# Two projections of a mixer as one product in seven parts, with the order of its neighbours changed: an encoder kernel on one Trainium2 core

## The chip, the core and the metric

One NeuronCore of a Trainium2 chip runs the whole program. The metric is the device time of one execution in microseconds. Abbreviations as in the profile: PE is TensorE (matmuls; PEld its weight loads), DVE VectorE, ACT ScalarE, POOL GpSimd, SP SyncE; POOL and SP issue the DMAs here. "L178" is line 178 of the kernel.

## What is computed

Two layers, each a half-step feed-forward part (FFN), a mixer, and a second FFN, on x of 512 tokens by 1024 channels, float32 (hidden width 2816). The mixer, cut to what matters:

```python
h = rms_norm(x)
z = h @ w_in                      # q, k, v, uf: 512 columns each; ga, gf: 1024 each
y_na = neighbourhood_attention(q, k, v, rpb) @ w_na_out     # 8 heads of 64
y_f  = real(fft2(uf per group of 128 channels, over positions and channels)) @ w_f_out
x = x + (sigmoid(ga + b0) * y_na + sigmoid(gf + b1) * y_f) @ w_o
```

## The kernel before

**Precision and products.** Every float32 operand of a matmul is split in a high and a low part of a rounded type, and a product is three matmuls: high by high, high by low, low by high (`mm3` L285 to L288; the low part is made by `split`: ACT copies the high part, L292 or L295, DVE subtracts, L293 or L296). A matmul of 128x512 has 128 rows of output channels or tokens and 512 columns. The FFNs and the mixer's gates multiply 2x2 blocks with seven products in place of eight (Strassen's scheme, `product`, L447, L448, L450): each product is 24 matmuls of 128x512 into two PSUM banks, and sums and differences of x's blocks and of the weights' blocks are its operands.

**The weight stream.** All weights lie in DRAM as granules of 128x1024 float32 (512 KB), in a list in the order of use (`stage_items`). `Stream.fetch` issues their loads on SP's queue eight ahead (L144); sums of two granules are made by a second DMA that adds, on POOL's queue (L146, L180), or by DVE (L160). `prep` then makes the high part on ACT (`whi`, L175, negated L170) and the low part on DVE (`wlo`, L178, L171), three buffers of each, two granules ahead of PE.

**The mixer before the change.** `Norm.quad` transposes x on PE and splits each chunk from PSUM (L295, L296). `proj_U` computes u (the 512 Fourier columns) as it stands for the first half of the tokens and in reversed order for the second half, with reversed copies of x's parts on ACT and DVE (L986, L987) as operands: 96 matmuls of 128x512. `proj_V`: 96 more. Between them 1/rms comes by integer start and three Newton steps on DVE (`rsqrt`, L304 to L309), and `spread` sends it to all partitions by DRAM as R; `constants` loads the Fourier matrices by POOL's queue. Then, in program order: the bias and shifted-v loads (SP), `four_pos` for four groups (12 matmuls each; DVE multiplies by the rotations L1048, L1049, adds and subtracts L1050, L1051, then the split into b), q and k of head pair 0 (`proj_T`, 24 matmuls each, times R on DVE L970, split), `four_ch` for four groups (6 matmuls each, two PSUM banks each; ACT evicts `fq` L1063, DVE combines to `fy` L1065 to L1067, split into y L1071, L1072), q of pair 1, then the attention of four head pairs.

`att_next(hp)` transposes the probabilities of the pair before (`att_trans`, L1140, split into p), does the scores of pair hp (`att_scores`, 24 small matmuls, L1104), adds the bias and finds the maximum on DVE (L1118), takes Exp on ACT (L1124), the reciprocal of the sum on DVE (L1127) and scales on ACT (L1131). `att_outs(hp)` multiplies the transposed probabilities by v. `f_some(n)` does n of the eight row blocks of y_f (12 matmuls of 128x512 each, L1202 evicts; the first four rows read one pair of weight granules, the others a second). The order of these calls is:

```python
four_pos x4; q0; k0; four_ch x4; q1
att_next(0); k1; q2;  att_next(1); k2; att_outs(0); q3
att_next(2); k3; att_outs(1); f_some(2)
att_next(3); f_some(2); att_outs(2); f_some(1); att_next(4); f_some(2); ...
```

**What sets the order.** PE runs in program order, in effect. The queues of DVE and ACT are ordered by a scheduler in the framework, which places the instructions by their program order and its own reckoning of when operands are ready; inside `manual_schedule` blocks they stand as written. Each queue is strict: an instruction that waits holds up all behind it. PSUM has eight banks, given out in turn.

Of the kernel before, what the change touches and what calls it, by code (L numbers as in the profile page):

```python
# [17 lines left out]
P = 128  # L18
# [22 lines left out]
def _granules():  # L41
# [7 lines left out]
    for l in range(L):  # L49
        for w in (1, 2):  # L50
# [36 lines left out]
def encoder_kernel(  # L87
# [95 lines left out]
    def stage_items():  # L183
# [5 lines left out]
        def strassen(s, name, idx, sizes, order, dma=False):  # L189
# [7 lines left out]
            for m in order:  # L197
                for g in range(len(sizes)):
# [13 lines left out]
                    else:  # L212
                        add(c)

# [15 lines left out]
        for l in range(L):  # L230
# [4 lines left out]
            for name, n in (("u", 4), ("v", 4), ("qk", 8), ("f", 4)):  # L235
                for g in range(n):
                    add(Raw((s, name, g)))
# [11 lines left out]
    class Stream:  # L249
        def __init__(self):  # L250
            self.items = stage_items()
            self.pos = self.loaded = self.prepped = 0
            self.stage = 0

# [6 lines left out]
        def prep(self, to):  # L261
            n = len(self.items)
            while self.prepped < min(to, n) and self.items[self.prepped].stage <= self.stage:
                self.fetch(self.prepped + FETCH)
# [4 lines left out]
        def enter(self, stage):  # L269
            self.stage = stage  # L270
            self.fetch(self.prepped + FETCH)
# [40 lines left out]
    class Norm:  # L312
# [105 lines left out]
        def rstd(self):  # L418
# [101 lines left out]
    def less(ps, t):  # L520
        for b in range(2):
            V.tensor_tensor(t[:, b, :], ps[b], t[:, b, :], ALU.subtract)  # L522

    def stage_ffn(norm, nxt, late):
# [27 lines left out]
        norm.tiles(1)  # L552
# [16 lines left out]
        acts = {1: (hx[0], lx[0], 0), 2: (hx[1], lx[1], 0), 3: (hx[1], lx[1], 256), 4: (*t4, 0)}  # L569

        def combine(m):

            if m == 5:
                V.tensor_tensor(raw[0, 0], raw[0, 0], raw[0, 1], ALU.subtract)
                acts[5] = parts(raw[0, 0], "t1")
            elif m == 7:
# [1073 lines left out]
```

## Time and profile before

| what | us |
|---|---|
| median of three runs (lowest, highest) | 1905.98 (1905.19, 1907.02) |
| the profiled execution | 1906.04 |
| span in its profile | 1904.2 |
| PE busy | 1891.7 |
| first matmul of u, layer 0 | 337.15 |
| end of scores of head pair 0, layer 0 | 408.45 |
| its first transpose | 419.56 |

The profile is one execution. Its page gives the busy time of each engine, the span in 40 slices, the DMA queues, the chain that ended last, and the costliest groups of instructions; the trace behind it answers more: the waits of an engine with what released it, the busy time in given stretches, the instructions of a stretch in order of time. A line such as "383.30 0.69 DVE L1048 ..." has the start, the duration, the engine, the line, the operation, and its output and inputs. Matmuls, and most instructions of DVE and ACT, begin before the one ahead has ended, so the price of one in a full queue is the step from one start to the next.

### The profile page before, as it was taken

The numbers are of one execution on the slowest core, as the hardware profiler recorded it, in microseconds if no ns is written. First come the engines' busy times: TensorE is split into PE (matmuls) and PEld (weight loads), VectorE is DVE, ScalarE is ACT, GpSimd is POOL, SyncE is SP. The second block draws the span as 40 slices with busy tenths as digits, with TensorE's granted clock in tenths as the row PEclk, the third lists the DMA queues.
The fourth block names the chain that finished last, engine by engine and source line by source line (L and its number), as shares of the span: only waits on it lengthen the run. The fifth ranks groups of instructions, "written<-read, shape, count | busy, mean of one in ns | idle before, by whom it ended". The sixth has DMA issues, their size and how long they took to land.

```text
span 1904.2 us, 25091 instructions
## 1 busy us (share of the span) xinstructions
PE 1891.7 (99%) x9189; PEld 1586.8 (83%) x9189; DVE 1602.4 (84%) x2000; ACT 1161.6 (61%) x1676; POOL 160.7 (8%) x198
## 2 busy tenths in 40 slices
PE   9999999999999999999999999999999999999998
PEld 7888888888888888888888888888888888888886
DVE  7877899586889987889997778995769899787899
ACT  6655665468566755566665556663675576555655
POOL 0101010000111010001010100100001101000010
PEclk9999999999999999999999999999999999999999
DMA  8776499323886776649877664992247867766594
GB/s 301 202 207 187 150 249 320 105 84 104 217 218 166 180 195 204 177 152 262 251 185 210 187 180 152 268 339 74 68 130 215 215 170 175 207 177 177 170 275 147
DMA packets 104636, 364.36 MB, mean 191 GB/s; under 512 B 12032, under 2 KB 12160, under 8 KB 104512
## 3 DMA queue, kind: packets, MB, share of 16 engines
q1 hardware_dynamic: 77568, 270.70, 40.1%
q0 software_dynamic: 26800, 92.04, 26.8%
q8 instruction: 72, 1.18, 0.2%
q14 instruction: 52, 0.43, 0.1%
q10 hardware_dynamic: 144, 0.02, 0.0%
HBM read 357.46 MB, written 2.11 MB: 189 GB/s over the span
## 4 chain that ended last, share of the span: by engine, by line
PE 95%; issue 2%; DMA 2%; DVE 1%; ACT 0%; POOL 0%; DVEq 0%; ACTq 0%; POOLq 0%; SPq 0%
PE A L447 9%; PE A L448 9%; PE A L450 9%; PE o L448 7%; PE o L447 7%; PE o L450 7%; PE ps L286 5%; PE ps L288 5%; PE ps L287 5%; PE B L448 4%; PE B L447 4%; PE B L450 4%; PE C L448 2%; PE C L447 2%; PE C L450 2%; PE tr L540 2%
## 5 line engine op out<-in xcount | busy, mean ns | idle before, releaser
L175 ACT ACTIVATE whi<-raw 128x1024 fp32r<-128x1024 f32 (+1 forms) x528 | 546.1, 1037 | 423.4 <-PE A L448 123.2
L178 DVE TENSOR_TENSOR wlo<-raw,whi 128x1024 fp32r<-128x1024 f32 (+1 forms) x528 | 627.3, 1193 | 191.2 <-ACT whi L175 186.5
L146 POOL DMA_DIRECT2D raw<-in_wst_dram x158 | 136.2, 873 | 1440.2 <-DMA raw<-in_wst_dram 674.7
L160 DVE TENSOR_TENSOR raw<-raw,raw 128x1024 f32<-128x1024 f32 (+1 forms) x146 | 172.6, 1191 | 1.2
L448 PE MATMUL A<-whi,xl 128*128 128x512 f32 x384 | 149.5, 389 | 0.0
L447 PE MATMUL A<-whi,xh 128*128 128x512 f32 x384 | 149.4, 389 | 0.0
L450 PE MATMUL A<-wlo,xh 128*128 128x512 f32 x384 | 110.5, 389 | 0.0
L170 ACT ACTIVATE whi<-raw 128x1024 fp32r<-128x1024 f32 (+1 forms) x79 | 81.6, 1036 | 40.2 <-PE A L448 12.4
L171 DVE SCALAR_TENSOR_TENSOR wlo<-raw,whi 128x1024 fp32r<-128x1024 f32 (+1 forms) x79 | 93.1, 1193 | 12.2 <-ACT whi L170 12.2
L633 ACT ACTIVATE th<-sn,rh 128x512 f32<-128x512 f32 x80 | 56.8, 714 | 69.4 <-DVE sn L522 69.4
L517 ACT ACTIVATE sn<-A 128x512 f32<-128x512 f32 x96 | 56.4, 589 | 51.3 <-PE A L450 51.2
L450 PEld LDWEIGHTS A<-wlo,xh 128*128 128x128 f32 x384 | 72.1, 188 | 15.0
L448 PEld LDWEIGHTS A<-whi,xl 128*128 128x128 f32 x384 | 72.1, 188 | 14.8
L447 PEld LDWEIGHTS A<-whi,xh 128*128 128x128 f32 x384 | 72.1, 188 | 14.8
L447 PE MATMUL B<-whi,t1h 128*128 128x512 f32 x192 | 76.2, 397 | 0.0
L447 PE MATMUL A<-whi,t3h 128*128 128x512 f32 x192 | 75.3, 392 | 0.4 <-ACT sn L517 0.4
L447 PE MATMUL C<-whi,xh 128*128 128x512 f32 x192 | 74.9, 390 | 0.0
L447 PE MATMUL A<-whi,t2h 128*128 128x512 f32 x192 | 74.9, 390 | 0.0
L448 PE MATMUL B<-whi,t1l 128*128 128x512 f32 x192 | 74.8, 390 | 0.0
L448 PE MATMUL A<-whi,t3l 128*128 128x512 f32 x192 | 74.8, 390 | 0.0
L448 PE MATMUL C<-whi,xl 128*128 128x512 f32 x192 | 74.7, 389 | 0.0
L448 PE MATMUL A<-whi,t2l 128*128 128x512 f32 x192 | 74.7, 389 | 0.0
(409 smaller groups left out, 4748.2 us busy)
## 6 DMA issues: line engine op xcount, KB each, us to landing
raw<-in_wst_dram SPq DMA_DIRECT2D x466, 512.0 KB, 5.4
raw<-in_wst_dram POOLq DMA_DIRECT2D x162, 512.0 KB, 7.9
raw<-in_wst_dram SPq DMA_DIRECT2D x30, 256.0 KB, 3.9
bm<-in_bias_dram SPq DMA_DIRECT2D x16, 384.0 KB, 6.0
vs<-v SPq DMA_DIRECT2D x12, 256.0 KB, 4.9
x<-in_xin_dram SPq DMA_DIRECT2D x4, 512.0 KB, 10.2
raw<-in_wst_dram POOLq DMA_DIRECT2D x8, 256.0 KB, 8.7
dft<-in_dft_dram POOLq DMA_DIRECT2D x8, 256.0 KB, 6.2
```

The source lines that it names most:

```text
L146: G.dma_start(out=self.t, in_=wst[GRAN_AT[self.plus]][:, 0 : self.n], accum_op=ALU.add)
L160: V.tensor_tensor(self.raw.t, self.raw.t, self.add.t, ALU.add)
L170: S.activation(hi, t, AF.Copy, scale=-1.0)
L171: self.last = V.scalar_tensor_tensor(lo, t, -1.0, hi.bitcast(F32), ALU.mult, ALU.subtract)
L175: S.activation(hi[:, cs], t[:, cs], AF.Copy)
L178: self.last = V.tensor_tensor(lo[:, cs], t[:, cs], hi[:, cs].bitcast(F32), ALU.subtract)
L286: PE.matmul(ps, lh, rh, start=start, stop=False, skip_group_check=again)
L287: PE.matmul(ps, lh, rl, start=False, stop=False, skip_group_check=again)
L288: PE.matmul(ps, ll, rh, start=False, stop=stop, skip_group_check=again)
L447: PE.matmul(ps, lh, rh, start=start, stop=False, skip_group_check=again)
L448: PE.matmul(ps, ll, rh, start=False, stop=False, skip_group_check=again)
L450: PE.matmul(ps, lh, rl, start=False, stop=stop, skip_group_check=again)
```

## The change

u and v become one product of 1024x1024 by 2x2 blocks in seven parts (`proj_UV`), in the order 1, 5, 6, 2, 3, 7, 4, where u is complete behind the sixth of them (product 7). Its weights are eight granules in blocks a, b, c, d, loaded sixteen times in all, in part by DMAs that add. The projections q0, k0, q1 and k1 stand between the products. The reversed second half of u comes from the finished u by a matmul with the mirror matrix (two per half, high and low part, copied on ACT with 1/rms of the reversed tokens) and not from reversed copies of x. 1/rms is taken by ACT's square root, a reciprocal and one Newton step on DVE; one value is loaded through the root at the start of the FFN's output stage in front of each mixer too. x's transposes are evicted raw on ACT, then split at once for a block. In `proj_UV` the order of ACT and DVE is fixed as written. Behind it four_pos, q2, the attention, k2 and four_ch follow in a new order, and the f rows are dealt out anew; `four_pos` and `four_ch` are no longer next to each other's q and k.

In the diff below the lines of `proj_U` and `proj_V` that go (they are printed above) and unchanged lines are left out.

```diff
                         add(d, a, then=b.key if dma else None)
                     else:
                         add(c)
+                for key in (behind or {}).get(m, ()):
+                    add(Raw(key))
         def out_sizes(c):
             return (1024, 512) if c == 0 else (1024, 1024)
             st += 1
             s = (l, 0)
             two = (1024, 1024)
-            for name, n in (("u", 4), ("v", 4), ("qk", 8), ("f", 4)):
-                for g in range(n):
-                    add(Raw((s, name, g)))
+            qk = [(s, "qk", g) for g in range(8)]
+            strassen(s, lambda q: "u" + q, 0, two, (1, 5, 6, 2, 3, 7, 4), True, behind={5: qk[0:1], 6: qk[1:2], 2: qk[2:3], 7: qk[3:4]})
+            for key in qk[4:] + [(s, "f", g) for g in range(4)]:
+                add(Raw(key))
             st += 1
             for g in range(2):
                 add(Raw((s, "n", 0, g)))
...
+            self.quad_high(i, j)()
+        def quad_high(self, i, j):
...
-            if not self.mix:
-                raw = self.raw[i, j] = slot(F32, "xr")
+            raw = self.raw[i, j] = slot(F32, "xr")
...
-                    if self.mix:
-                        split(hq[:, kt, :], lq[:, kt, :], tr[:, k, :], self.gain(4 * i + kt))
-                    else:
-                        S.activation(raw[:, kt, :], tr[:, k, :], AF.Copy, scale=self.gain(4 * i + kt))
-            if not self.mix:
-                split(hq, lq, raw)
+                    S.activation(raw[:, kt, :], tr[:, k, :], AF.Copy, scale=self.gain(4 * i + kt))
+            S.activation(hq, raw, AF.Copy)
+            return lambda: V.tensor_tensor(lq, raw, hq.bitcast(F32), ALU.subtract)
...
-            if self.mix:
-                pc = bank()
-                PE.matmul(pc[:, 0:2], mirror, self.r[:, 3:1:-1], start=True, stop=True)
-                self.rflip = small("rflip", 2)
-                V.tensor_copy(self.rflip, pc[:, 0:2])
-                return
...
+        def rstd_steps(self):
+            ms, q, t = small("ms", 4), small("sq", 4), small("rt", 4)
+            r = self.r = small("r", 4)
+            V.tensor_tensor(ms, self.ssq[:, 0:4], self.ssq[:, 4:8], ALU.add)
+            V.tensor_scalar(ms, ms, 1.0 / D, EPS, ALU.mult, ALU.add)
+            S.activation(q, ms, AF.Sqrt)
+            yield
+            V.reciprocal(r, q)
+            V.tensor_tensor(t, r, r, ALU.mult)
+            V.scalar_tensor_tensor(t, t, -0.5, ms, ALU.mult, ALU.mult)
+            V.scalar_tensor_tensor(r, t, 1.5, r, ALU.add, ALU.mult)
+            yield
+        def flip(self):
+            pc = bank()
+            PE.matmul(pc[:, 0:2], mirror, self.r[:, 3:1:-1], start=True, stop=True)
+            self.rflip = small("rflip", 2)
+            V.tensor_copy(self.rflip, pc[:, 0:2])
...
-            V.tensor_tensor(t[:, b, :], ps[b], t[:, b, :], ALU.subtract)
+            res = V.tensor_tensor(t[:, b, :], ps[b], t[:, b, :], ALU.subtract)
+        return res
+    def combos(norm, t4):
+        norm.tiles(0)
+        norm.tiles(1)
+        raw, hx, lx = norm.raw, norm.h, norm.l
+        acts = {1: (hx[0], lx[0], 0), 2: (hx[1], lx[1], 0), 3: (hx[1], lx[1], 256)}
+        if t4:
+            acts[4] = (*t4, 0)
+        def combine(m):
+            p, a, b, op = {
+                5: ((0, 0), (0, 0), (0, 1), ALU.subtract),
+                7: ((0, 1), (0, 1), (1, 1), ALU.subtract),
+                6: ((0, 0), (1, 1), (0, 0), ALU.add),
+                4: ((1, 0), (1, 0), (0, 0), ALU.subtract),
+            }[m]
+            V.tensor_tensor(raw[p], raw[a], raw[b], op)
+            yield
+            if m != 4 or not t4:
+                acts[m] = (slot(F32R, f"t{m}h"), slot(F32R, f"t{m}l"), 0)
+            h, l, _ = acts[m]
+            S.activation(h, raw[p], AF.Copy)
+            yield
+            V.tensor_tensor(l, raw[p], h.bitcast(F32), ALU.subtract)
+            yield
+        return acts, combine
...
-        if late:
+        if late or nxt.mix:
...
-                    nxt.quad(0, 1)
+                    if nxt.mix:
+                        nxt.low01 = nxt.quad_high(0, 1)
+                    else:
+                        nxt.quad(0, 1)
...
+        mir = mp.tile([P, P], F32R, tag="mir", name=nm("mir"), bufs=1)
...
+            def out():
+                t = tmp(s="q")
+                V.tensor_tensor(t, ps, R, ALU.mult)
+                hi, lo = hilo("q")
+                if scale is None:
+                    S.activation(hi, t, AF.Copy)
+                else:
+                    S.activation(hi, t, AF.Copy, scale=scale)
+                def rest():
+                    if scale is None:
+                        V.tensor_tensor(lo, t, hi.bitcast(F32), ALU.subtract)
+                    else:
+                        V.scalar_tensor_tensor(lo, t, scale, hi.bitcast(F32), ALU.mult, ALU.subtract)
+                    return hi, lo
+                return rest
+            return out
+        def proj_UV():
+            acts, combine = combos(norm, None)
+            ws.depth = 8
+            with tc.manual_schedule(engines={mybir.EngineType.DVE, mybir.EngineType.Activation}):
+                steps = {m: combine(m) for m in (5, 6, 7, 4)}
+                def step(m, n=1):
+                    for _ in range(n):
+                        next(steps[m])
+                step(5)
+                pa = pair("A")
+                product(pa, acts[1], K4, True, hook=lambda: step(5, 2))
+                root = norm.rstd_steps()
+                next(root)
+                ws.items[ws.prepped + 1].summed()
+                next(root)
+                norm.spread(R)
+                ws.prep(ws.pos + 3)
+                low10 = norm.quad_high(*norm.due.pop(0))
+                s1 = snap(pa)
+                norm.low01()
+                def second():
+                    low10()
+                    step(6, 2)
+                pb = pair("B")
+                product(pb, acts[5], K4, True, hook=second)
+                sb = snap(pb)
+                step(6)
+                q0 = proj_T(DH**-0.5)
+                step(7, 2)
+                product(pa, acts[6], K4, False, again=True, hook=lambda: step(7))
+                s2 = snap(pa)
+                k0 = proj_T(None)
+                step(4, 2)
+                q0 = q0()
+                step(4)
+                pc = pair("C")
+                product(pc, acts[2], K4, True)
+                q[0] = q0()
+                q1 = proj_T(DH**-0.5)
+                k0 = k0()
+                less(pc, s1)
+                k[0] = k0()
+                product(pb, acts[3], K4, False, again=True)
+                q1 = q1()
+                less(pb, s2)
+                uh, ul = slot(F32R, "uh", (2, T)), slot(F32R, "ul", (2, T))
+                S.activation(uh, s2, AF.Copy)
+                q[1] = q1()
+                norm.flip()
+                product(pa, acts[7], K4, False, again=True, hook=lambda: V.tensor_tensor(ul, s2, uh.bitcast(F32), ALU.subtract))
+                constants()
+                S.activation(mir, mirror, AF.Copy)
+                flipped = []
                 for c in range(2):
...
+                    pm = bank()
+                    PE.matmul(pm, mir, uh[:, 1 - c, :], start=True, stop=False)
+                    PE.matmul(pm, mir, ul[:, 1 - c, :], start=False, stop=True)
+                    t = tmp(s="uf")
+                    S.activation(t, pm, AF.Copy, scale=norm.rflip[:, c : c + 1])
+                    flipped.append(t)
+                less(pa, sb)
+                k1 = proj_T(None)
+                us, rest = [[], []], []
                 for c in range(2):
...
+                    for op in (ALU.add, ALU.subtract):
+                        w = tmp(s="ue")
+                        V.scalar_tensor_tensor(w, s1[:, c, :], norm.r[:, c : c + 1], flipped[c], ALU.mult, op)
+                        hi, lo = hilo("u")
+                        S.activation(hi, w, AF.Copy)
+                        us[c].append((hi, lo))
+                        rest.append((lo, w, hi))
+                        if len(rest) > 1:
+                            l_, w_, h_ = rest.pop(0)
+                            V.tensor_tensor(l_, w_, h_.bitcast(F32), ALU.subtract)
+                vt = [None] * 4
+                def v_out(c, src):
+                    t = vt[c] = slot(F32R, "v", (2, T))
+                    split(t[:, 0, :], t[:, 1, :], src, norm.r[:, c : c + 1])
+                product(pa, acts[4], K4, False, again=True)
+                l_, w_, h_ = rest.pop(0)
+                V.tensor_tensor(l_, w_, h_.bitcast(F32), ALU.subtract)
+                k1 = k1()
+                v_out(2, sb[:, 0, :])
+                k[1] = k1()
+                v_out(3, sb[:, 1, :])
+            ws.depth = FETCH
+            for b in range(2):
+                v_out(b, pa[b])
+            return us, vt
...
+            o.append(hilo("o"))
...
-        u = proj_U()
-        vt = proj_V()
+        u, vt = proj_UV()
+        def f_rows():
+            for i in range(2):
+                yield from fill(yf, fs, i)
+        f_fill = f_rows()
+        def f_some(n):
+            for _ in range(n):
+                next(f_fill)
+        for g in range(4):
+            four_pos(g)
+        proj_q(2)
...
             nc.sync.dma_start(out=t[64:128].bitcast(F32), in_=vt[s + 1][0:64].bitcast(F32))
             vs.append(t)
         vch = {i: (t[:, 0, :], t[:, 1, :]) for i, t in ((0, vt[0]), (1, vs[0]), (2, vt[1]), (3, vs[1]), (4, vt[2]), (5, vs[2]), (6, vt[3]))}
-        for g in range(4):
-            four_pos(g)
-        proj_q(0)
-        proj_k(0)
+        att_next(0)
+        bias_for(1)
+        proj_k(2)
         for g in range(4):
             four_ch(g)
-        proj_q(1)
-        def f_rows():
-            for i in range(2):
-                yield from fill(yf, fs, i)
-        f_fill = f_rows()
-        def f_some(n):
-            for _ in range(n):
-                next(f_fill)
-        for hp in range(3):
-            att_next(hp)
-            bias_for(hp + 1)
-            proj_k(hp + 1)
-            if hp:
-                att_outs(hp - 1)
-            if hp < 2:
-                proj_q(hp + 2)
+        att_next(1)
+        bias_for(2)
+        att_outs(0)
+        proj_q(3)
+        proj_k(3)
+        att_next(2)
+        bias_for(3)
         f_some(2)
+        att_outs(1)
+        f_some(1)
...
         next(first)
         att_next(4)
         swap_pools(0)
-        f_some(2)
+        f_some(1)
         next(first)
         att_outs(3)
```

More of the change, by code (lines that the diff above doesn't have):

```diff
@@ L67, in _granules @@
                 s = (l, 0)
-                for name, n in (("u", 4), ("v", 4), ("qk", 8), ("f", 4)):
+                for q in "abcd":
+                    for g in range(2):
+                        put(s, "u" + q, 0, g)
+                for name, n in (("qk", 8), ("f", 4)):
                     for g in range(n):
@@ L187, in add, with strassen @@
             items.append(Item(*a, stage=st, **k))
-        def strassen(s, name, idx, sizes, order, dma=False):
+        def strassen(s, name, idx, sizes, order, dma=False, behind=None):
             def key(q, g):
@@ L253, in __init__ @@
             self.stage = 0
+            self.depth = FETCH
         def fetch(self, to):
@@ L567, in plain @@
             late_low(parts)
[L569 removed]
+        acts, steps_of = combos(norm, t4)
         def combine(m):
[L573 to L576, printed above, removed]
[L577 to L584 removed]
+            for _ in steps_of(m):
+                pass
         if first:
@@ L954, in constants @@
                 tc.keep_in_program_order(G.dma_start(out=rots[hl], in_=src))
-        def wide():
-            wh, wl = ws.next()
-            for k in range(2):
-                c = slice(k * T, (k + 1) * T)
-                yield wh[:, c], wl[:, c]
         def proj_T(scale):
@@ L1557, in _weights @@
             wst[GRAN_AT[s, "qk", i]] = z
-        for name, m in (("u", u), ("v", v)):
-            for i in range(4):
-                wst[GRAN_AT[s, name, i]] = _wide(m, (2 * i, 2 * i + 1), 0)
         def four(name, i, w1, c1, w2, c2):
@@ L1568, in _weights @@
         wo = g["mix_w_o"][l]
+        four("u", 0, u, 0, v, 0)
         four("w", 0, wo, 0, wo, T)
```

77 lines of the change are left out of this document (4 added, 73 removed).

## The prediction

> **What bounds the kernel now.** The page first: span, busy time by engine, the chain that ended last.
>
> ```profile
> span 1904.2 us, 25091 instructions
> ...
> PE 1891.7 (99%) x9189; PEld 1586.8 (83%) x9189; DVE 1602.4 (84%) x2000; ACT 1161.6 (61%) x1676; POOL 160.7 (8%) x198
> ...
> PE 95%; issue 2%; DMA 2%; DVE 1%; ACT 0%; POOL 0%; DVEq 0%; ACTq 0%; POOLq 0%; SPq 0%
> ```
>
> Then the waits of PE:
>
> ```profile
> PE ps L132 <- ACT warm L129: 2.7, 1, 2.7
> PE A L447 <- ACT sn L517: 0.4, 2, 0.2
> ```
>
> TensorE is the bound everywhere, and after its start it waits 0.4 us in all. So a matmul removed is worth its whole time, and every new wait of PE is a loss. Next, five stretches around layer 0's mixer (the end of the FFN before it to 337; u and v to 382; Fourier stages and q, k to 408; the first attention):
>
> ```profile
> 310.00:337.00 27.00, 27.00 (x129) 22.56 (x129) 26.67 (x35) 17.48 (x31) 0.55 (x1) 1.00 1.01 385
> 337.00:360.00 23.00, 23.00 (x108) 19.18 (x107) 10.99 (x33) 8.79 (x19) 4.55 (x8) 1.00 0.42 139
> 360.00:382.00 22.00, 22.00 (x99) 18.23 (x99) 11.53 (x16) 10.01 (x14) 0.00 (x0) 1.00 0.04 13
> 382.00:408.00 26.00, 26.00 (x163) 22.88 (x163) 23.66 (x50) 12.21 (x20) 0.00 (x0) 1.00 0.44 123
> 408.00:425.00 17.00, 17.00 (x105) 14.27 (x103) 12.33 (x33) 12.65 (x33) 0.00 (x0) 1.00 0.14 46
> ```
>
> Columns: length, then PE, PEld, DVE, ACT and POOL busy, granted clock, DMA share, GB/s. PE is full in each. DVE has half its time free before 382 and 2.3 us of 26 behind it: that is the place with no slack, and the change moves work towards it.
>
> **Prices** (start, duration; the step between back-to-back starts is the price, since a duration overhangs the next start):
>
> ```profile
> 58.65 0.91 PE B L450 x4
> ...
> 406.83 1.62 PE ps L1104 x24
> 408.45 0.43 PE ps L286
> ...
> 419.56 1.75 PE ps L1140 x16
> ```
>
> ```profile
> 398.33 0.28 PE L286 MATMUL ps<-b,ch 128*128 128x258 f32 x1
> ...
> 401.20 0.40 PE L286 MATMUL ps<-xh,whi 128*128 128x512 f32 x1
> ```
>
> A 128x512 matmul costs 0.2267 us (0.23 rounded up; 0.91 for four), so a projection or a product of 24 costs 5.44; a score stage of 24 matmuls 1.62; 16 transposes 1.75; four_ch, 24 matmuls of about 256 columns, 2.87 or 0.12 each, so four_pos (48) 5.74.
>
> ```profile
> 383.30 0.69 DVE L1048 TENSOR_TENSOR m<-ps,rot 128x512 f32<-128x512 f32 x1
> 383.91 0.68 DVE L1049 TENSOR_TENSOR m<-ps,rot 128x512 f32<-128x512 f32 x1
> 384.51 1.22 DVE L178 TENSOR_TENSOR wlo<-raw,whi 128x1024 fp32r<-128x1024 f32 x1
> 385.64 0.42 DVE L1050 TENSOR_TENSOR bt<-m,m 128x256 f32<-128x256 f32 x1
> 385.98 0.42 DVE L1051 TENSOR_TENSOR bt<-m,m 128x256 f32<-128x256 f32 x1
> 386.31 0.69 DVE L1048 TENSOR_TENSOR m<-ps,rot 128x512 f32<-128x512 f32 x1
> ...
> 401.14 0.42 DVE L1065 TENSOR_TENSOR fy<-ps,fq 128x256 f32<-128x256 f32 x1
> ...
> 401.90 0.06 DVE L1062 MEMSET fq<- 128x1 f32 x1
> ...
> 409.81 0.42 DVE L1118 CUSTOM_DVE_ANT_0 s<-ps,bm 128x256 f32<-128x256 f32 x1
> 410.15 0.08 DVE L1118 DVE_READ_ACCUMULATOR2_ANT nmx<- 128x1 f32 x1
> ```
>
> On DVE: a low part or product of 128x512 costs 0.60, wlo 1.13, the halves of bt 0.34 each, fy 0.76, a score operation 0.34.
>
> ```profile
> 399.27 0.36 ACT L1063 ACTIVATE fq<-ps 128x255 f32<-128x255 f32 x1
> 399.53 0.62 ACT L292 ACTIVATE q<-q 128x512 fp32r<-128x512 f32 x1
> 400.05 0.37 ACT L1063 ACTIVATE fq<-ps 128x255 f32<-128x255 f32 x1
> ...
> 410.33 0.51 ACT L1124 ACTIVATE s<-s,nmx 128x256 f32<-128x256 f32 x1 [2.04 <-DVE nmx L1118]
> ...
> 417.49 0.62 ACT L292 ACTIVATE q<-q 128x512 fp32r<-128x512 f32 x1
> ```
>
> On ACT: fq 0.26, a high part of 128x512 0.52, and one attention's 8 Exps and 8 scalings 7.16 us from the first Exp.
>
> **The change, part by part.**
>
> *Removed.* u and v take 96 matmuls of 128x512 each now (8 row blocks x 4 x 3 parts); afterwards 7 x 24 = 168 and 4 by the mirror matrix. Per layer 192 - 172 = 20 go; the two instruction orders agree (7473 against 7433, every other shape as often as before). 40 x 0.2267 = **-9.07 us**.
>
> *The seven products* get 16 granules by DMA in place of 8: 4.2 MB more per layer, 11 us at the 385 GB/s of the full queue in the first row above. That row has no room, the two behind it leave 13 + 21 us of DMA time free, and the stream asks eight granules ahead: I take it as hidden; uncovered it would cost at most those 11 us. Combinations of x and of weights land on DVE and ACT, which are free for 22 and 26 us of these 45; 8 more wlo and whi take 9.0 and about 8, four combinations with their parts about 9 and 4. It fits in sum; taking the three queues in order, each operation behind its inputs, the tightest joins (second half of the sixth combination, k0's weights, u's low part) have 0.1 to 0.5 us to spare. I take 0, range 0 to 2 us per layer. 1/rms by ACT's root, q0, k0, q1, k1 between the products, and the constants' DMAs (on POOL's queue, behind R) cost PE nothing: their readers come 3 us or more later.
>
> *The first attention.* Here I expect the loss. Let P be the end of the seventh product. PE's order behind it: four_pos 5.74, q2 5.44, scores(0) 1.62, k2 5.44, four_ch 2.87, then the transposes of attention 0. Unhindered PE is there at P + 21.1.
>
> DVE reaches P with u's parts just done, one low part open, and then has, in the order of its instructions: that low part and k1 by R (1.2), a wlo (1.13), four low parts of v and one of k1 (5 x 0.60 = 3.0), four_pos 4 x (0.60 + 0.60 + 0.34 + 0.34) = 7.5, three low parts of b 1.8, q2 by R 0.6: 15.2. So its first score operation is at P + 15.2, though PE had the scores at P + 12.8. Two low parts (1.2) stand between it and the other seven.
>
> ACT must load a table ahead of the first Exp, because the root was used since. The only load in mid-kernel now:
>
> ```profile
> 1786.36 0.62 ACT L170 ACTIVATE whi<-raw 128x512 fp32r<-128x512 f32 x1
> 1786.99 1.28 ACT L813 ACT_TABLE_LOAD   x1
> 1788.28 0.20 ACT L813 ACTIVATE sq<-ones 128x1 f32<-128x1 f32 x1
> ```
>
> It takes 1.28, most of it beside those two low parts. First Exp at about P + 17.1 (now 0.52 behind the first score operation); + 7.16 = P + 24.2; a high part of k2 0.52 and the first fq 0.26: **P + 25.0**. Only then can PE go on, for two reasons: the transposes read the scaled probabilities, and four_ch's eight tiles fill all eight PSUM banks, which come free by fq (ACT) and fy (DVE), queued behind the probabilities. The waits in PE's order say so: the transposes' four tiles wait for ACT, ACT, DVE, ACT and the scores of attention 1 for DVE, ACT, DVE, DVE.
>
> From P + 24.8 DVE has, ahead of the first low part of the transposed probabilities: a low part of k2 0.6, four fy 3.0, four low parts of y 2.4, a wlo 1.13, two score operations 0.7, then that low part 0.6 = 8.4. So the first output matmul of attention 0 (its second one needs the low part) starts at **P + 33.3**. PE unhindered: 21.1 + 1.75 + 1.62 = P + 24.5. **Stall 8.8 us per layer**, in pieces: about 3.9 ahead of the transposes, the rest between them and the output.
>
> Why not today: behind scores(0) PE has k1 and q2, 419.56 - 408.45 = 11.1 us, and four_ch was through at 401.20; the chain first score to last scaling is 417.5 - 409.8 = 7.7 and is covered. After the change the cover is 5.44 + 2.87 = 8.3 us, and the chain starts 2.4 us late, carries the table load and is followed by eight evictions.
>
> *f rows.* Three of the eight rows of f stand before attention 3 in place of two, so the second pair of f's weights is due one row earlier, 7.5 us behind the start of attention 2's transposes. ACT makes its high part behind four Exps (0.49 each) that start 4.7 us behind that: 4.7 + 2.0 + 0.95 = 7.6; DVE's low part 1.13 later, 8.8, against 7.9 wanted. About **1.2 us per layer**.
>
> *The sum.* -9.07 + 2 x (8.8 + 1.2) = +10.9; with the finer steps of the walk (8.9) +11.1. The profiled execution took 1906.04, the span 1904.2 and 1.84 around it; the median 1905.98 is 0.06 away. 1906.04 + 11.1 = **1917.2 us**. DVE 4% quicker or slower over its 33 us shifts the stall by 1.4 per layer: 1914.3 to 1920.
>
> **Beside the rows: the load of a table.** The Trainium skill, "ScalarE: Activation LUTs", section "What ACT_TABLE_LOAD costs", gives about 1283 ns for the load and some 1380 ns of drain, 2.66 us in all. The rows above show the 1.28 but no drain: the load starts as the activation ahead of it ends. By the page my estimate would be 1.4 us per layer more, 1920; I stay with the row.
>
> **Rivals.**
>
> *A: the gain arrives.* DVE's and ACT's queues behind P keep up, PE does not wait: 1906.04 - 9.07 = 1897.0. For it: DVE is free for half of the time before P, and u is done a product earlier. Against it: the 15.2 us are work that reads the seventh product, four_pos or q2. It decides if fq and the probabilities are done by P + 21.1, 3.9 us earlier than I find. 13%.
>
> *B: the stall is half as long* (evictions in another order than I take, about 4.5 per layer): 1906.04 - 9.07 + 9 = 1906. 8%.
>
> *C: the clock falls in the gap.* From P + 21.1 to P + 33.3 PE has 3.4 us of work. At the start of this trace, behind 2.73 us without work, matmuls of 512 columns ran at half speed:
>
> ```profile
> 2.73 4.02 PE ps L132 x9
> ...
> 6.75 0.43 PE cl L447
> ...
> 8.79 0.23 PE cl L448
> ```
>
> From 2.73 to 8.79 fourteen matmuls, 3.2 us of work, took 6.06: 2.9 lost. Were that paid again behind the gap, part of it inside the stall, 1.5 to 2.9 per layer: 1920 to 1923. For it: one piece is 3.9 us long. Against it: no wait in mid-kernel today shows it (0.4 us in all), and the gap is broken by transposes and scores. 20%. The Trainium skill, "TensorE: Matmul & The Clock Gate", section "What's actually happening", has the clock at half after an idle window of about 3.4 us and back after as long a busy one; that rule speaks for this rival and the slow start agrees with it.
>
> *D: the seven products stall too,* at the tight joins, 1 to 2 us per layer: 1919 to 1921. 9%.
>
> **How the numbers follow.** My forecast 1917.2 (1912 to 1921) has 50%, A 13%, B 8%, C 20%, D 9%. Range 1905 to 1924: below it A, above it a clock loss with late joints. About 0.2% is what a measurement can tell from no change, 3.8 us: faster below 1902.2 (A: 13%), same to 1909.8 (B: 8%), slower 79%.
>
> **What would show it.** Right: PE's busy time near 1882.6; waits of PE for transposes (ps from s), for scores of attention 1 and for p's low part, about 9 us in each mixer, released by ACT and DVE; a granted clock of 1.00 through it. Wrong: PE at the transposes without a wait (A); PE waits in the seven products (D); matmuls of 0.43 behind the gap (C). A missing table load ahead of the Exps would take 0.4 us off; a queue order other than that of the instructions would undo the sum.

## The result, and the profile after

The changed kernel takes 1924.51 us (median of four runs, 1923.36 to 1926.87), the kernel before, beside it, 1905.59 (1904.72 to 1907.02): 1.0100 times, 95% interval 1.0083 to 1.0118, some 19 us slower. That is the side that was forecast, 7.3 us above the forecast of 1917.2 and 0.5 above the end of the range.

The profiled execution took 1926.87. Its page: span, busy times, the chain that ended last.

```profile
span 1925.1 us, 25076 instructions
...
PE 1896.5 (99%) x9149; PEld 1587.7 (82%) x9149; DVE 1638.6 (85%) x1992; ACT 1193.8 (62%) x1712; POOL 171.5 (9%) x210
...
PE 83%; DVE 6%; issue 4%; ACT 4%; DMA 3%; POOL 0%; DVEq 0%; ACTq 0%; POOLq 0%; SPq 0%
```

There are 40 PE instructions fewer, as counted, yet PE is busy 4.8 us longer: part of its work ran at a lower clock. DVE and ACT have 10% of the chain, where they had 1%. What PE waited for (line, releaser: us in total, times, longest):

```profile
PE ps L1230 <- ACT fq L1154: 6.6, 2, 3.3
...
PE ps L293 <- DVE fq L1153: 2.0, 2, 1.0
PE ps L294 <- DVE wlo L181: 1.5, 2, 0.8
PE o L470 <- DVE c4l L300: 1.4, 1, 1.4
PE A L470 <- DVE t6l L571: 1.1, 2, 1.0
PE ps L294 <- DVE p L300: 0.9, 2, 0.5
```

The transposes (L1230) wait for four_ch's eviction, the f rows for wlo, the output for p's low part, twice each: once per layer, at the places of the prediction. One more, 1.0 us per layer, stands ahead of the last tile of four_ch itself (L293, released by `fq` L1153). The seventh product of layer 0 ends at 399.28 (P), 62.40 us after the stage began. From there to the first matmul of the gates (500.97) it is 101.69 us, in layer 1 101.47. Unhindered it would be 89.08: the kernel before takes 492.51 - 381.67 = 110.84 without a wait, and has four projections of 5.44 more in it. So **12.6 us in layer 0 and 12.4 in layer 1** are lost behind P. The stretch of layer 0 by pieces (length; PE, PEld, DVE, ACT, POOL busy; granted clock; DMA share; GB/s):

```profile
399.28:420.40 21.12, 21.12 (x142) 18.63 (x140) 20.90 (x50) 12.37 (x24) 0.00 (x0) 1.00 0.35 79
420.40:424.80 4.40, 0.67 (x4) 0.42 (x3) 1.34 (x5) 4.40 (x15) 0.00 (x0) 1.00 0.43 161
424.80:431.70 6.90, 6.24 (x33) 5.51 (x34) 6.38 (x20) 4.16 (x9) 0.00 (x0) 0.51 0.00 0
431.70:435.10 3.40, 2.69 (x18) 2.07 (x18) 3.39 (x10) 2.99 (x8) 0.00 (x0) 1.00 0.00 0
435.10:438.50 3.40, 3.40 (x18) 3.40 (x18) 3.11 (x17) 2.88 (x11) 0.00 (x0) 0.50 0.15 19
```

Four things are to be read: DVE is full for the first 21 us while PE runs on; then ACT alone is full (the probabilities) and PE idle; then DVE is full again (the evictions, then p); and the granted clock is at half in two of the pieces, 10.2 us in all. The instructions that carry the chain, in order of time, first ACT and DVE, then PE:

```profile
415.23 0.41 DVE L1208 CUSTOM_DVE_ANT_0 s<-ps,bm 128x256 f32<-128x256 f32 x1
...
433.38 2.48 DVE L300 TENSOR_TENSOR p<-ps,p 128x512 fp32r<-128x512 f32 x4
```

```profile
415.34 0.63 ACT L1015 ACTIVATE q<-q 128x512 fp32r<-128x512 f32 x1
415.99 1.28 ACT L1214 ACT_TABLE_LOAD   x1
417.29 0.51 ACT L1214 ACTIVATE s<-s,nmx 128x256 f32<-128x256 f32 x1
...
424.95 0.36 ACT L1154 ACTIVATE fq<-ps 128x255 f32<-128x255 f32 x1
```

```profile
425.37 4.04 PE L1230 MATMUL ps<-ident,s 128*128 128x128 f32 x16 [3.30 <-ACT fq L1154]
429.33 3.77 PE L1194 MATMUL ps<-q,q 64*128 64x256 f32 x24
433.28 0.38 PE L293 MATMUL ps<-p,v 128*128 128x256 f32 x1 [0.17 <-ACT p L299]
434.12 0.38 PE L294 MATMUL ps<-p,v 128*128 128x256 f32 x1 [0.46 <-DVE p L300]
```

The 16 transposes take 4.0 us and the 24 score matmuls 3.8, where they took 1.75 and 1.62 before.

### The profile page after: what moved, and what is told of

It is laid out like the page before. It is cut to its first block, busy times and chain, and to the rows that moved or that the text cites. A ratio compares the mean times of both kernels' runs of the same rounds, so it can differ in the third digit from the quotient of the medians.

```text
span 1925.1 us, 25076 instructions
## 1 busy us (share of the span) xinstructions
PE 1896.5 (99%) x9149; PEld 1587.7 (82%) x9149; DVE 1638.6 (85%) x1992; ACT 1193.8 (62%) x1712; POOL 171.5 (9%) x210
## 4 chain that ended last, share of the span: by engine, by line
PE 83%; DVE 6%; issue 4%; ACT 4%; DMA 3%; POOL 0%; DVEq 0%; ACTq 0%; POOLq 0%; SPq 0%
PE A L470 9%; PE A L469 9%; PE A L472 9%; PE o L470 6%; PE o L469 6%; PE o L472 6%; PE B L469 4%; PE B L470 4%; PE B L472 4%; DMA raw<-in_wst_dram 3%; PE ps L294 2%; PE ps L295 2%; PE C L470 2%; PE ps L293 2%; PE C L469 2%
## 5 line engine op out<-in xcount | busy, mean ns | idle before, releaser
L178 ACT ACTIVATE whi<-raw 128x1024 fp32r<-128x1024 f32 (+1 forms) x536 | 553.3, 1037 | 379.9 <-PE A L470 119.3
L181 DVE TENSOR_TENSOR wlo<-raw,whi 128x1024 fp32r<-128x1024 f32 (+1 forms) x536 | 636.1, 1193 | 168.1 <-ACT whi L178 165.7
L149 POOL DMA_DIRECT2D raw<-in_wst_dram x166 | 144.4, 896 | 1389.1 <-DMA raw<-in_wst_dram 724.1
L174 DVE SCALAR_TENSOR_TENSOR wlo<-raw,whi 128x1024 fp32r<-128x1024 f32 (+1 forms) x83 | 98.0, 1194 | 15.2 <-ACT whi L173 14.0
L173 ACT ACTIVATE whi<-raw 128x1024 fp32r<-128x1024 f32 (+1 forms) x83 | 85.8, 1037 | 36.5 <-PE o L470 12.8
L470 PE MATMUL C<-whi,xl 128*128 128x512 f32 x208 | 81.0, 389 | 0.0
L470 PE MATMUL B<-whi,xl 128*128 128x512 f32 x208 | 81.0, 389 | 0.0
L469 PE MATMUL B<-whi,xh 128*128 128x512 f32 x208 | 80.9, 389 | 0.0
L472 PE MATMUL B<-wlo,xh 128*128 128x512 f32 x208 | 59.8, 389 | 0.0
L472 PE MATMUL C<-wlo,xh 128*128 128x512 f32 x208 | 59.8, 389 | 0.0
L470 PE MATMUL A<-whi,t6l 128*128 128x512 f32 x136 | 53.2, 391 | 1.1 <-DVE t6l L571 1.1
L469 PE MATMUL B<-whi,t5h 128*128 128x512 f32 x136 | 54.2, 399 | 0.0
## 6 DMA issues: line engine op xcount, KB each, us to landing
x<-in_xin_dram SPq DMA_DIRECT2D x4, 512.0 KB, 10.2
```

Of the source, the lines that this page charges most:

```text
L149: G.dma_start(out=self.t, in_=wst[GRAN_AT[self.plus]][:, 0 : self.n], accum_op=ALU.add)
L173: S.activation(hi, t, AF.Copy, scale=-1.0)
L174: self.last = V.scalar_tensor_tensor(lo, t, -1.0, hi.bitcast(F32), ALU.mult, ALU.subtract)
L178: S.activation(hi[:, cs], t[:, cs], AF.Copy)
L181: self.last = V.tensor_tensor(lo[:, cs], t[:, cs], hi[:, cs].bitcast(F32), ALU.subtract)
L469: PE.matmul(ps, lh, rh, start=start, stop=False, skip_group_check=again)
```

## The experiments

**Theory 1**: the place of four_ch and of the projections leaves attention 0's chain on ACT and DVE (scores, Exps, evictions, p) too little PE work beside it; PE waits, and a half clock follows that costs time too. **Rivals**: it is the half clock alone or not at all; the backlog that the seven products leave on DVE; the table load. Each run is given beside the kernel before on the same chip, 1905.6 to 1906.2 us. "Lost" is the time from P to the gates less PE's own work there, layer 0 and 1. The last column is what the profiled execution shows between P and the gates.

| run | us | lost, us | half clock inside, us per layer |
|---|---|---|---|
| changed kernel | 1924.51 | 12.6, 12.4 | 10.2 |
| filler in the gap | 1924.05 | 13.6, 12.9 | 6.8 |
| evictions first | 1918.05 | 10.0, 9.5 | 6.8 |
| q3 ahead of four_ch | 1916.52 | 9.8, 9.6 | 6.8 |
| both | 1917.13 | 9.9, 9.0 | 6.8 |
| f rows as before | 1925.11 | 13.9, 12.9 | 13.7, 10.2 |
| no root | 1926.26 | 12.9, 13.0 | 10.2 |
| four_ch first | 1915.61 | 7.8, 7.8 | 0 |

**Filler in the gap.** Behind the fourth four_ch PE gets work that nothing reads:

```diff
             mm3(p2[:, 0:256], ch[:, 1, 0, :], ch[:, 1, 1, :], bh[:, 256:512], bl[:, 256:512], True, True)
+            if g == 3:
+                for _ in range(24):
+                    PE.matmul(p2[:, 256:512], ch[:, 1, 0, :], bh[:, 256:512], start=True, stop=True)
```

> The changed kernel with 24 idle matmuls (128x256, about 2.9 us) behind the fourth four_ch, into unused columns of its PSUM tile: work that nothing reads, in the place where PE waits longest. Theory 1 (the half clock behind the gap costs time of its own, about 3 us per layer): no half clock behind the gap, transposes back to 1.75 us, time 1918 to 1921 against 1924.5. Rival (the half clock lies inside the stall and costs nothing): 1924 to 1925.

1924.05: the rival's time; theory 1 had both its time and its sign (no half clock) wrong. The granted clock:

```profile
421.20:424.30 3.10, 3.07 (x26) 2.86 (x24) 0.33 (x2) 3.10 (x11) 0.00 (x0) 1.00 0.17 67
424.30:432.80 8.50, 5.65 (x41) 4.55 (x41) 8.14 (x26) 5.34 (x12) 0.00 (x0) 0.97 0.00 0
432.80:439.60 6.80, 6.54 (x28) 6.06 (x29) 4.99 (x19) 5.52 (x18) 0.00 (x0) 0.53 0.21 62
```

The gap is filled and the transposes run at full clock, but DVE sets the first output, at P + 34.0 as in the changed kernel. So the half clock over the transposes, which this run does not have, had cost nothing. The waits are now in pieces, and a half clock comes all the same, 8.2 us later counted from P, over the outputs, where nothing hides it: from the second output matmul (433.45) to the end of them (438.53) it takes 5.08 us where 23 steps of 0.12 are 2.75, 2.3 lost; in the changed kernel it is 1.6 (4.33 us). A half clock inside the stall is free; what of it falls behind the stall costs half its length.

**Evictions first.** Priority for the evictions of four_ch's first three groups, and 11 temporary tiles in place of 8 so that they have room:

```diff
-            return mp.tile([P, T], dt, tag="tmp", name=nm(s), bufs=8)
+            return mp.tile([P, T], dt, tag="tmp", name=nm(s), bufs=11)
...
+            with tc.high_priority() if g < 3 else nullcontext():
                 qs = tmp(s="fq")
...
```

> The changed kernel with the evictions of the first three four_ch groups put ahead of the probabilities in the queues of ACT and DVE (priority), and 11 temporary tiles in place of 8 so that they have room. Theory 1 (the low part of the transposed probabilities stands behind eight evictions on DVE): the transposes start about as late (P + 25 to 26), the first output matmul follows within 4 us and not 9, time 1912 to 1916. Rival (the wait is for the probabilities alone, the order of the evictions does not matter): 1924.

1918.05, less than theory 1 wanted. The output begins at P + 32.9, only 1.1 us earlier: the first half of the transposes now begins without a wait, but the second half waits until P + 27.0 for the probabilities, since the evictions stand between the Exps.

```profile
PE ps L1231 <- ACT s L1222: 6.1, 2, 3.1
```

The order shifts the work; its sum stays. The rest of the gain is the half clock, which now lies mostly inside the stall: the outputs take 3.51 us (432.77 to 436.28), 0.6 more than their 2.87. The run changes priority and the number of tiles together, and no run has one of them alone.

**More cover.** q3 ahead of four_ch:

```diff
         att_next(0)
         bias_for(1)
         proj_k(2)
+        proj_q(3)
         for g in range(4):
             four_ch(g)
...
         att_outs(0)
-        proj_q(3)
         proj_k(3)
```

> The changed kernel with q3 moved ahead of four_ch, so that 13.8 us and not 8.3 us of PE work stand between the scores and the transposes of attention 0 (and 5.4 us less between those of attention 1). Theory 1 (too little PE work beside a chain of fixed length): the 3.3 us wait ahead of the transposes goes and the half clock with it, some 4 us of stall stay behind the transposes, 1 to 2 us come new at attention 1: 1911 to 1916. Rival (DVE and ACT are simply full there, the place does not matter): 1923 to 1925.

1916.52, 0.5 above theory 1's range; its other sign, that the half clock goes, failed. The wait of 3.3 us is gone, no wait of PE at the attention is over 0.9 us, and still the clock falls:

```profile
PE ps L1230 <- ACT fq L1154: 2.9, 6, 0.6
...
PE ps L1194 <- DVE fq L1153: 1.8, 2, 0.9
PE ps L1194 <- DVE fy L1158: 1.6, 2, 0.8
```

```profile
425.10:432.70 7.60, 4.84 (x35) 3.56 (x34) 7.36 (x21) 4.21 (x9) 0.00 (x0) 0.99 0.00 0
432.70:439.50 6.80, 6.41 (x28) 6.05 (x29) 5.76 (x22) 5.16 (x15) 0.00 (x0) 0.51 0.09 11
```

DVE is full (7.36 of 7.60) ahead of the outputs: cover helps, but 5.44 us more of it do not reach to the end of DVE's chain.

**Both** edits together.

> The changed kernel with both: q3 ahead of four_ch (more PE work beside attention 0's chain) and the evictions of four_ch ahead of the probabilities (11 temporary tiles). Theory 1 (cover too short, and evictions in front of the transposed probabilities): the two gains add, 2 to 3 us of stall per layer left and no half clock, 1902 to 1908. Theory 2 (what counts is the sum of ACT and DVE work between the scores and the first output, wherever it stands): the second gain is small beside the first, and the half clock stays: 1912 to 1916.

1917.13: the signs of theory 2, 1.1 us above its range. PE now waits amid the scores of attention 1, until DVE has combined the fourth group of four_ch, and the half clock stays:

```profile
PE ps L1195 <- DVE fy L1159: 7.7, 2, 3.8
```

From 424.86 on DVE has no pause. The fourth group's `fy` stands in its queue behind three low parts of y, two of weights and one of q:

```profile
427.86 1.89 DVE L1164 TENSOR_TENSOR y<-fy,y 128x512 fp32r<-128x512 f32 x3
429.66 1.22 DVE L181 TENSOR_TENSOR wlo<-raw,whi 128x1024 fp32r<-128x1024 f32 x1
430.80 0.69 DVE L1021 SCALAR_TENSOR_TENSOR q<-q,q 128x512 fp32r<-128x512 f32 x1
431.41 1.22 DVE L181 TENSOR_TENSOR wlo<-raw,whi 128x1024 fp32r<-128x1024 f32 x1
...
432.55 0.42 DVE L1157 TENSOR_TENSOR fy<-ps,fq 128x256 f32<-128x256 f32 x1
```

So what counts here is how much ACT and DVE have to do between the scores and the first output, and how much PE has beside it.

**f rows as before.**

```diff
         att_outs(1)
-        f_some(1)
...
         swap_pools(0)
-        f_some(1)
+        f_some(2)
```

> The changed kernel with the f rows dealt out as before the change (two ahead of attention 3, two behind attention 4). Theory 1: the wait of PE for the second pair of f's weights (0.8 us and what lies around it) goes, 1.2 us per layer: 1922. Rival (the row only moves, the stall with it, or attention 3 loses its cover): 1924 to 1925.

1925.11: the rival, at the end of its range. The wait for wlo (0.8 us per layer) goes, but attention 2's chain has lost 2.72 us of cover, and the scores of attention 3 now wait for p's low parts (0.5 and 0.2 us in layer 0). This profile also has 3.4 us more of half clock in layer 0 (13.7). The 1.2 us were there, but this place of the row did not win them.

**The new tail alone.** The kernel before, with four_ch behind attention 0's scores (calls joined in a line; the loop over the head pairs, in whose place the added lines stand, goes):

```diff
         for g in range(4):
             four_pos(g)
         proj_q(0)
         proj_k(0)
-        for g in range(4):
-            four_ch(g)
         proj_q(1)
...
+        att_next(0); bias_for(1); proj_k(1)
+        for g in range(4):
+            four_ch(g)
+        att_next(1); bias_for(2); att_outs(0); proj_q(2); proj_k(2)
+        att_next(2); bias_for(3); proj_q(3); proj_k(3); att_outs(1)
         f_some(2)
```

> The kernel before, u and v as they were, with the new place of four_ch alone: four_pos, q0, k0, q1, attention 0, k1, four_ch, attention 1 and so on, q2, k2, q3 and k3 behind. Theory 1 (the place of four_ch between the scores and the transposes makes the stall, about 5 us per layer without the backlog and the table load, and a half clock may follow): 1914 to 1923. Rival (the stall comes from what the seventh product leaves to DVE and ACT, the place alone costs little): 1905 to 1909.

1924.23, 1.2 above theory 1's range, ratio 1.0096 (1.0081 to 1.0111): slower by as much as the whole change, without the seven parts, their backlog or a table load. From four_pos to the gates it takes 120.86 us in layer 0 (501.90 - 381.04) where it took 110.84, in layer 1 119.64 for 110.83. The waits have the releasers of the changed kernel's, none is over 1.0 us, and the clock falls to half for 6.8 us in layer 0 and 3.4 in layer 1.

```profile
PE ps L1140 <- ACT fq L1063: 3.2, 4, 1.0
...
PE ps L1104 <- DVE fq L1062: 1.8, 2, 0.9
PE ps L1104 <- DVE fy L1067: 1.7, 2, 0.8
PE ps L286 <- DVE p L293: 1.2, 2, 0.6
```

This settles the place: the order behind u and v loses 10.0 and 8.8 us per layer by itself. The changed kernel loses 2.6 and 3.6 more there. 1.3 of them in each layer are the f rows (below); what the rest owes to the backlog of the seven parts no run separates.

**four_ch first.** The changed kernel with four_ch ahead of the attention (calls joined in a line):

```diff
+        proj_k(2)
+        for g in range(4):
+            four_ch(g)
         att_next(0); bias_for(1)
-        proj_k(2)
-        for g in range(4):
-            four_ch(g)
+        proj_q(3); proj_k(3)
         att_next(1); bias_for(2)
-        att_outs(0); proj_q(3); proj_k(3)
+        f_some(1); att_outs(0); f_some(1)
         att_next(2); bias_for(3)
-        f_some(2); att_outs(1); f_some(1)
+        f_some(1); att_outs(1); f_some(1)
...
         att_next(3)
-        f_some(2)
+        f_some(1)
         att_outs(2)
```

> The changed kernel with four_ch ahead of the attention (four_pos, q2, k2, four_ch, attention 0, q3, k3, attention 1) and the f rows two by two between the attentions. Theory 1 (the product in seven parts is worth its 9.1 us, the loss is all in the order behind it): the wait of 3.3 us and the half clock go, the new gaps of 8.3 us of PE work at attentions 1 to 3 cost 1 to 1.5 us each: 1900 to 1906. Rival (the seven parts leave DVE so much that any order stalls): over 1912.

1915.61: the rival's range, but not its cause. The stage of the seven products takes 62.36 us, no half clock comes and PE reaches the first transposes 0.7 us late, so the seven parts do not bring every order to a stall. But 7.8 us per layer are lost, 6.7 of them at attentions 1 to 3, whose transposes and scores take 6.34, 5.45 and 5.33 us in layer 0 where the kernel before takes 3.46 (419.39 to 422.85), mostly in pauses too short to be listed as waits. ACT is full or nearly so there (6.40 of 6.40 us, 5.25 of 5.45, 5.12 of 5.33), here at attention 1:

```profile
432.00:438.40 6.40, 4.80 (x42) 3.42 (x40) 3.82 (x8) 6.40 (x16) 0.00 (x0) 1.00 0.02 5
```

The kernel before has 74.9 us of PE work from the scores of attention 0 to the last f row (406.76 to 481.63). Three projections of 5.44 were moved ahead of that, so 58.5 us are left, and they take 65.9 (418.78 to 484.70).

**No root.** 1/rms by three Newton steps on DVE (`rsqrt`) in `proj_UV`, and no root at the start of the FFN's output stage:

```diff
-                root = norm.rstd_steps()
...
+                norm.r = rsqrt(ms, 4)
...
-        if late or nxt.mix:
+        if late:
```

> The changed kernel with 1/rms by three Newton steps on DVE again and no root on ACT, so that no table is loaded ahead of the Exps. Theory 1 (the load of 1.28 us lies mostly beside DVE's two low parts): first Exp 0.4 us earlier in each layer, 1923 to 1924.5. Rival (the load delays the whole chain by its length or more, 1.3 to 2.7 us per layer): 1919 to 1922.

1926.26, above both ranges. No table is loaded; the first Exp comes at P + 16.6 and not P + 18.0, but the second, which waits for DVE, only 0.55 us earlier than before, and so the transposes. DVE's extra steps cost that elsewhere: PE has new waits for q by R (0.8 us per layer) and for a low part of x (1.4 us in both layers together). Without the load 12.9 and 13.0 us are lost behind P, so the load is not what makes the loss.

**Two and three projections between the parts.** To get the cover back, fewer projections stand between the products and more at the attention. In the first, k0 and q1 leave their places, k0 takes that of k1, and behind P come

```python
four_pos x4; q1; k1; four_ch x4; att_next(0); q2; k2
att_next(1); att_outs(0); q3; k3; att_next(2); f_some(2); att_outs(1); f_some(1)
att_next(3); f_some(1); att_outs(2); f_some(2); att_next(4); ...
```

> The product in seven parts kept, but only q0 and one k (k0, ahead of the seventh product) between its parts; behind it four_pos, q1, k1, four_ch, attention 0, q2, k2, attention 1, output 0, q3, k3, attention 2 and three f rows between the last ones, so that each chain has 10 us or more of PE work beside it. Theory 1 (the 9.1 us are real, the loss is cover alone): no half clock, 1 to 4 us per layer left, from joins of the seven parts which now lie closer: 1899 to 1905. Rival (the seven parts fill DVE and ACT so far that what is won at the attention is lost at their joins): 1908 to 1915.

1924.62, above both ranges. Behind P 4.6 us are lost in each layer (104.54 less 99.96), and at the products 9.4 in layer 0 (60.68 from start to P; the changed kernel's 62.40 less its wait of 0.2 and two projections is 51.3), a half clock of 6.8 us among them:

```profile
PE B L469 <- ACT whi L178: 6.7, 2, 4.6
```

Product 3 waits for its weights: they are granules of product 6 to which a second DMA adds (L183), issued when product 6's parts are made. ACT finds the second of them landed only at 374.27:

```profile
356.07 0.56 POOL L462 DMA_DIRECT2D R<-row  x1 [9.44 <-DMA row<-r]
356.62 0.94 POOL L183 DMA_DIRECT2D raw<-in_wst_dram  x1
...
357.74 1.60 POOL L183 DMA_DIRECT2D raw<-in_wst_dram  x1
```

In the changed kernel these DMAs are issued no earlier (from 357.60), but product 3 begins at 376.36 and does not wait: the projections between the parts were the cover of the adding DMA. Here its issues stand behind that of R, which waited 9.4 us for its row; no run tried to issue them sooner. With three between (q0; k0 ahead of product 3; q1 ahead of the last) and four_pos, k1, q2, four_ch, attention 0, k2, q3, attention 1, k3, output 0, one f row behind P:

> The product in seven parts with three projections between its parts (q0 behind the second, k0 ahead of the part whose weights came late in the run with two, q1 ahead of the last) and five behind: four_pos, k1, q2, four_ch, attention 0, k2, q3, attention 1, k3, output 0, one f row, attention 2, three f rows around output 1, attention 3. Theory 1 (ACT needs some 66 us from the scores of attention 0 to the end of the attention, as it took in the run with four_ch first; PE has 63.8 us of work there in this order): 2 to 3 us per layer lost there, 0 to 2 at the seven parts, no half clock: 1901 to 1907. Rival (the weights of the third-last part come late whatever stands ahead of it, 5 us per layer and a half clock behind): 1912 to 1920.

1915.03, in the rival's range, but by losses at both places: behind P 4.3 us per layer (98.84 less 94.52), at the products 5.6 in layer 0 (with 3.4 us of half clock) and 2.5 in layer 1.

No order tried kept the 9.1 us; none was quicker than the kernel before. The seven parts with all projections behind them were not tried.

## Why the prediction failed by its size

- **What PE sheds** was nearly right: 40 matmuls went, and of the 4.53 us per layer 4.0 came in layer 0. u and v take 62.40 us less four projections, 40.64, where they took 44.68 (336.99 to 381.67); 0.2 of the difference is a wait.
- **The seven products** at 0: right in layer 0 (0.2 us of waits); layer 1 waited 1.0 us for the sixth combination's low part, a join named as tight and inside its 0 to 2.
- **The first attention** happened where and as it was told. The clock times behind P:

| step | forecast | measured |
|---|---|---|
| first score operation | 15.2 | 15.95 |
| first Exp | 17.1 | 18.0 |
| first fq begins | 24.7 | 25.7 |
| first output matmul | 33.3 | 34.0, its second 34.8 |

  The chain was priced 1.0 us too short at `fq` and 1.4 at the second output, which was forecast 0.12 behind the first: DVE came to u's last low part 0.4 us behind P, and v's low parts take 0.66, not 0.60, each.
- **The f rows**: 1.2 forecast; row 4 and 5 took 6.83 us for 5.57, 1.26.
- **The step that failed is the choice in "How the numbers follow"**: the half clock was kept apart as rival C, with 20%, and the sum has no term for it. It came in both layers, 10.2 us each. Most lay inside the stall, but its second part fell on the outputs of attention 0: from the second of them (434.12) to their end (438.45) it takes 4.33 us where 23 steps of 0.12 are 2.75, so 1.6 lost, inside C's price of 1.5 to 2.9. C's argument against itself ("the gap is broken by transposes and scores") was wrong: the waits in the run with q3 ahead were no longer than 0.9 us, and the clock fell. Of the signs, a clock of 1.00 and PE's busy time near 1882.6 did not come (0.50; 1896.5), and the slow matmuls behind the gap came.
- **The second step, a term mis-sized,** is DVE's and ACT's chain to the first outputs: P + 33.4 forecast for the second output, 34.8 measured. With the 1.6 that is 3.0 us in layer 0 up to the end of attention 0's outputs; behind them 0.4 less is lost than was reckoned. Without either of the two, some 3 us for both layers, the time would have stayed inside the range.
- Together: 10.0 forecast per layer behind P, 12.5 measured, so 5.0 of the 7.3 us; the join in layer 1 is 1.0. In the profiled execution, 2.4 us above the median, 3.1 us more were lost behind the second mixer (467.55 us from the gates to the end before, 470.63 after), where a row of R came late (DVE waits 2.5 us for it) and the last output waited 1.4 for c4l. What that is in the median run, and why R comes later there, stays open.
- **The explanation "why today not"** was too narrow: it looked at attention 0 alone. The projections that the change moves ahead were cover for the later attentions too, which fits that moving four_ch away again mended only about half of the loss (1915.61).

## What to carry to other kernels

When PE is full, independent matmuls such as projections are not only work: they are the cover of the chains on the other engines, and moving them forward to cover a new place uncovers the old one. Sum the cover over a whole stage ahead of pricing single joins (PE work from the first score to the last f row: 74.9 us before, 58.5 with four_ch first, which then took 65.9). And price a stall with the half clock behind it from the start.

## What the runs showed of the hardware

The granted clock had two values, 1.00 and 0.50, and changed only in steps. In each of the twelve traces every change lies a whole multiple of 3.413 us behind the trace's first one: in the changed kernel the clock is full from 8.40, half from 424.83 (122 steps on), full from 431.65, half from 435.07. The first change lies at 5.65 to 8.57 us, differently in each trace, so the steps lie differently against the kernel from one execution to another. Each half clock at the mixers lasted 3.4 us or 6.8 us.

What brings it down is no single long wait. The tail alone has no wait over 1.0 us at the mixers, and three steps in a row with PE busy 2.13, 2.21 and 2.57 of 3.41 us were followed by half clock. With four_ch first, one such step (2.02) between nearly full ones was not:

```profile
411.98:415.39 3.41, 2.13 (x17) 1.69 (x15) 1.35 (x6) 3.41 (x9) 0.00 (x0) 1.00 0.02 9
415.39:418.81 3.42, 2.21 (x17) 1.92 (x18) 3.27 (x11) 1.84 (x6) 0.00 (x0) 1.00 0.00 0
418.81:422.22 3.41, 2.57 (x21) 2.00 (x20) 3.31 (x12) 1.85 (x4) 0.00 (x0) 1.00 0.00 0
422.22:425.63 3.41, 2.97 (x13) 2.67 (x13) 3.41 (x10) 2.58 (x8) 0.00 (x0) 0.50 0.00 0
```

```profile
431.38:434.80 3.42, 3.35 (x21) 2.23 (x19) 0.93 (x3) 3.42 (x12) 0.00 (x0) 1.00 0.06 25
434.80:438.21 3.41, 2.02 (x24) 1.57 (x23) 2.87 (x6) 3.41 (x7) 0.00 (x0) 1.00 0.02 5
438.21:441.62 3.41, 3.27 (x16) 2.80 (x17) 3.41 (x11) 1.65 (x4) 0.00 (x0) 1.00 0.00 0
```

In the changed kernel one step with 2.69 busy (from 431.65), right behind a half clock, was enough for the next. The runs do not give the threshold. With waits of PE of 0.4 us in all after the start, the kernel before never showed a half clock at the mixers. "TensorE: Matmul & The Clock Gate" of the Trainium skill, section "What's actually happening", speaks of an idle window of about 3.4 us; the length fits these steps, but the drop needs no idle stretch of that length: here the measurement decides.

The table load took 1.28 us and the Exp followed 0.02 us later (417.29 behind 415.99 + 1.28), with no drain.
